# A streaming softmax: loads and stores in two queues without a fixed order, and four slots of twelve rows in place of six of eight

## The chip, the cores and the metric

The kernel runs on one core of one Trainium2 chip. The metric is the time of one execution in microseconds (us) on the device. The core has several engines with their own instruction streams: here VectorE (DVE in the profile), ScalarE (ACT) and SyncE (SP), which only issues transfers and waits. Transfers between the main memory (HBM) and the on-chip memory (SBUF, 128 partitions) are issued by an engine into its queue and carried out by the core's 16 DMA engines.

## The reference

The input is 32 x 512 rows of 1024 float32 numbers, 64 MiB, and a temperature of 0.5. Each row is replaced by its softmax:

```python
scaled = x / temperature
shifted = scaled - np.max(scaled, axis=-1, keepdims=True)
exp_x = np.exp(shifted)
return (exp_x / np.sum(exp_x, axis=-1, keepdims=True)).astype(np.float32)
```

Every number is read once and written once: 67.11 MB in, 67.11 MB out.

## The kernel before

The 16384 rows are dealt over the 128 partitions, 128 rows to each. A *row* below means one row in every partition: 128 x 1024 float32, 4 KiB in each partition. The data stand in one tile, `ring`, with room for 48 rows (`RING`, line 14), 192 KiB in each partition. A load brings `LOADS[i]` rows (line 10): 16 loads of 8 rows, 4096 KB each, so the ring has six slots. In each partition a load is one contiguous piece of 32 KiB, in memory and on the chip (`dram`, line 103). A store writes the same piece back (`STORES`, line 12). All work is done in place in the ring.

The computation goes by groups of four rows (`GROUP`, line 16), two groups to a load. For a group g:

- `maximum` (line 109): VectorE waits for the load, if g is the first group of it, and takes the largest number of each row (line 113).
- `shift` (line 120): VectorE multiplies the four maxima by -2, the bias of the exponential (line 123).
- `exponential` (line 127): ScalarE computes exp(2x + bias) of the four rows, one instruction for each, and sums them as it goes (line 131).
- `invert` (line 141): VectorE takes the reciprocals of the four sums (line 144).
- `divide` (line 146): VectorE multiplies the four rows by them (line 150), and counts up the semaphore `scaled`.

VectorE's order is written out at the end: maximum and shift of group g, then invert and divide of group g-1. So the last division of a piece comes behind the first maximum of the next piece, which waits for the next load.

All transfers are issued by SyncE, in an order that `_queue` (line 31) writes out ahead of time. It begins with six loads, one for each slot. From then on load i needs the slot of an earlier piece, and so must wait until the store of that piece has landed (line 165 behind the waits on `stored`). Ahead of such a load the list has the stores up to that piece and `AHEAD` = 2 further ones, each of which waits for the division of its last group (line 171 behind the wait on `scaled`). In the steady part store and load alternate in the one queue. After the last load come the remaining stores, and SyncE then waits until all have landed (line 176).

Of the kernel before, what the change touches and what calls it, by code (L numbers as in the profile page):

```python
# [1 line left out]

# [4 lines left out]

LOADS = [8] * 16  # L10

STORES = [[8]] * 16

RING = 48

GROUP = 4

AHEAD = 2


def _places(loads, ring):
    places, p = [], 0
    for k in loads:
        if p + k > ring:
            p = 0
        places.append(p)
        p += k
    return places


def _queue(loads, stores, places, ahead):

    flat = [(i, n) for i, ks in enumerate(stores) for n in range(len(ks))]
    last = {i: n for n, (i, _) in enumerate(flat)}
    order, given = [], 0
    for i, k in enumerate(loads):
        over = [
            b
            for b in range(i)
            if places[b] < places[i] + k and places[i] < places[b] + loads[b]  # L40
        ]
        after = max((last[b] for b in over), default=-1)
        while given <= after + ahead and after >= 0 and flat[given][0] < i:
            order.append(("store", given, None))
            given += 1
        order.append(("load", i, after))
    order += [("store", n, None) for n in range(given, len(flat))]
    return order


@with_exitstack
def kernel(
    ctx: ExitStack,
    tc: tile.TileContext,
    x: bass.AP,
    temperature: bass.AP,
    out: bass.AP,
):
    nc = tc.nc
    f32 = mybir.dt.float32  # L60
    scale = 1.0 / float(temperature)
    extreme = mybir.AluOpType.max if scale > 0 else mybir.AluOpType.min

    P = 128
    xf = x.flatten_outer_dims()
    of = out.flatten_outer_dims()
    n, d = xf.shape
    assert sum(LOADS) * P == n

    places = _places(LOADS, RING)  # L70
    first = [sum(LOADS[:i]) for i in range(len(LOADS))]
    total = sum(LOADS)

    pool = ctx.enter_context(tc.tile_pool(name="data", bufs=1))
    ring = pool.tile([P, RING, d], f32, name="ring")
    top = pool.tile([P, total], f32, name="top")
    bias = pool.tile([P, total], f32, name="bias")
    sums = pool.tile([P, total], f32, name="sums")
    recip = pool.tile([P, total], f32, name="recip")


    parts = []
    for i, ks in enumerate(STORES):
        j = 0
        for k in ks:
            parts.append((i, places[i] + j, first[i] + j, k))
            j += k
        assert j == LOADS[i]

    groups, part_end = [], []  # L90
    for i, s, r, k in parts:
        for a in range(0, k, GROUP):
            groups.append((i, s + a, r + a, min(GROUP, k - a)))
        part_end.append(len(groups))

    loaded = [tc.alloc_semaphore(f"loaded{i}") for i in range(len(LOADS))]
    stored = [tc.alloc_semaphore(f"stored{i}") for i in range(len(parts))]
    topped, biased, summed, inverted, scaled = (
        tc.alloc_semaphore(name)
        for name in ("topped", "biased", "summed", "inverted", "scaled")  # L100
    )

    def dram(t, r, k, i):

        block = t[P * first[i] : P * (first[i] + LOADS[i]), :]
        block = block.rearrange("(p k) d -> p k d", p=P, k=LOADS[i])
        return block[:, r - first[i] : r - first[i] + k, :]

    def maximum(g):
        i, s, r, k = groups[g]  # L110
        if g == 0 or groups[g - 1][0] != i:
            nc.vector.wait_ge(loaded[i], 16)
        nc.vector.tensor_reduce(  # L113
            out=top[:, r : r + k],
            in_=ring[:, s : s + k, :],
            axis=mybir.AxisListType.X,
            op=extreme,
        ).then_inc(topped, 1)

    def shift(g):  # L120
        i, s, r, k = groups[g]
        nc.vector.wait_ge(topped, g + 1)
        nc.vector.tensor_scalar_mul(  # L123
            bias[:, r : r + k], in0=top[:, r : r + k], scalar1=-scale
        ).then_inc(biased, 1)

    def exponential(g):
        i, s, r, k = groups[g]
        nc.scalar.wait_ge(biased, g + 1)
        for a in range(k):  # L130
            ins = nc.scalar.activation(  # L131
                ring[:, s + a, :],
                ring[:, s + a, :],
                mybir.ActivationFunctionType.Exp,
                bias=bias[:, r + a : r + a + 1],
                scale=scale,
                accum_out=sums[:, r + a : r + a + 1],
            )
        ins.then_inc(summed, 1)

    def invert(g):
        i, s, r, k = groups[g]
        nc.vector.wait_ge(summed, g + 1)
        nc.vector.reciprocal(recip[:, r : r + k], sums[:, r : r + k]).then_inc(inverted, 1)  # L144

    def divide(g):
        i, s, r, k = groups[g]
        nc.vector.wait_ge(inverted, g + 1)
        for a in range(k):
            ins = nc.vector.tensor_scalar_mul(  # L150
                ring[:, s + a, :], in0=ring[:, s + a, :], scalar1=recip[:, r + a : r + a + 1]
            )
        ins.then_inc(scaled, 1)

    done_to = -1
    with tc.tile_critical():  # L156

        for kind, i, after in _queue(LOADS, STORES, places, AHEAD):
            if kind == "load":
                for b in range(after + 1):  # L160
                    if b > done_to:
                        nc.sync.wait_ge(stored[b], 16)
                done_to = max(done_to, after)
                s, r, k = places[i], first[i], LOADS[i]
                nc.sync.dma_start(
                    out=ring[:, s : s + k, :], in_=dram(xf, r, k, i)
                ).then_inc(loaded[i], 16)
            else:
                l, s, r, k = parts[i]
                nc.sync.wait_ge(scaled, part_end[i])  # L170
                nc.sync.dma_start(
                    out=dram(of, r, k, l), in_=ring[:, s : s + k, :]
                ).then_inc(stored[i], 16)
        for b in range(len(parts)):
            if b > done_to:
                nc.sync.wait_ge(stored[b], 16)

        for g in range(len(groups)):
            exponential(g)


        for g in range(len(groups) + 1):
            if g < len(groups):
                maximum(g)
                shift(g)
            if g > 0:
                invert(g - 1)
                divide(g - 1)


# [1 line left out]
_INS = ['x', 'temperature']  # L192
_OUTS = [((32, 512, 1024), 'float32')]

_NUMBERS = {'temperature': 0.5}


# [26 lines left out]
```

## Time and profile before

Six runs took 321.31 to 323.24 us, with a median of 321.93. The profiled execution took 322.32 us; its span, from the first to the last instruction, is 320.5 us.

| what | value |
|---|---|
| profiled execution, span | 322.32 us, 320.5 us |
| VectorE busy | 235.4 us (73%) |
| ScalarE busy | 149.6 us (47%) |
| DMA queue q1 | 134.22 MB, 97.8% of 16 engines' span |
| maximum, 4 rows (line 113) | 32 of 4415 ns |
| exponential, one row (line 131) | 128 of 1137 ns |
| division, one row (line 150) | 128 of 749 ns |
| load, from issue to landing | 16, median 49.3 us |
| store, from issue to landing | 16, median 40.4 us |

Busy time of an engine counts its computing instructions. The share of a DMA queue is the time its packets took on the 16 DMA engines together, against 16 times the span. From issue to landing counts also the time in which a transfer stands in the queue behind others.

### The profile page before, as it was taken

How to read it: one execution, taken by the hardware profiler on the slowest of the kernel's cores; microseconds unless marked ns; L12 is line 12 of the kernel's file. 1: busy time of each engine (PE TensorE's matmuls, PEld its weight loads, DVE VectorE, ACT ScalarE, POOL GpSimd, SP SyncE). 2: the span in 40 equal slices, each digit the busy share in tenths (PEclk: the TensorE clock that was granted, in tenths of full speed). 3: DMA queues.
4: the chain of work that ended last, by engine and by line, in shares of the span. 5: the costliest groups of instructions: out<-in, count | busy, mean ns of one | idle time of the engine just before them, and what ended most of it. 6: DMA issues, size and time to landing. Idle time of an engine off the chain costs nothing.

```text
span 320.5 us, 568 instructions
## 1 busy us (share of the span) xinstructions
DVE 235.4 (73%) x224; ACT 149.6 (47%) x257; POOL 0.2 (0%) x4
## 2 busy tenths in 40 slices
DVE  0399999999996957939679395893948949498300
ACT  1076666665555551635526255262552625546000
POOL 0000000000000000000000000000000000000000
DMA  8999999999999999999999999999999999999992
GB/s 323 417 438 438 417 454 422 380 439 450 409 450 425 425 417 433 442 417 438 425 425 454 413 433 434 425 442 425 425 447 417 433 433 433 438 438 417 450 417 94
DMA packets 4612, 134.25 MB, mean 419 GB/s; under 512 B 512, under 2 KB 512, under 8 KB 512
## 3 DMA queue, kind: packets, MB, share of 16 engines
q1 hardware_dynamic: 4608, 134.22, 97.8%
q14 instruction: 4, 0.03, 0.0%
HBM read 67.11 MB, written 67.11 MB: 419 GB/s over the span
## 4 chain that ended last, share of the span: by engine, by line
DMA 55%; DVE 30%; another core or an unknown queue 5%; ACT 3%; issue 0%; SPq 0%
DMA ring<-in_x_dram 32%; DMA out_dram<-ring 24%; DVE top L113 18%; DVE ring L150 11%; ACT ring L131 3%; DVE bias L123 1%; DVE recip L144 0%; SPq L219 0%; SPq L156 0%
## 5 line engine op out<-in xcount | busy, mean ns | idle before, releaser
L131 ACT ACTIVATE ring<-ring,bias 128x1024 f32<-128x1024 f32 x128 | 145.4, 1137 | 146.6 <-DVE bias L123 146.6
L113 DVE TENSOR_REDUCE top<-ring 128x4 f32<-128x4096 f32 x32 | 141.3, 4415 | 60.4 <-DMA ring<-in_x_dram 60.4
L150 DVE TENSOR_SCALAR ring<-ring,recip 128x1024 f32<-128x1024 f32 x128 | 87.7, 749 | 1.1
L131 ACT ACTIVATION_READ_ACCUMULATOR ring<-ring,bias 128x1 f32 x128 | 23.9, 187 | 0.0
L144 DVE RECIPROCAL recip<-sums 128x4 f32<-128x4 f32 x32 | 5.5, 171 | 2.0 <-ACT ring L131 2.0
L123 DVE TENSOR_SCALAR bias<-top 128x4 f32<-128x4 f32 x32 | 5.4, 170 | 1.1
L131 ACT ACT_TABLE_LOAD x1 | 1.3, 1283 | 0.9 <-SPq L156 0.9
L205 POOL MEMSET const-bfloat16-1.0<- 128x1 bf16 x1 | 0.1, 101 | 0.0
L205 POOL MEMSET const-uint8-127<- 128x1 uint8 x1 | 0.1, 101 | 0.0
L205 POOL MEMSET const-float32-0.0<- 128x1 f32 x1 | 0.1, 98 | 0.2 <-issue 0.2
L205 POOL MEMSET const-float32-1.0<- 128x1 f32 x1 | 0.1, 98 | 0.0
## 6 DMA issues: line engine op xcount, KB each, us to landing
ring<-in_x_dram SPq DMA_DIRECT2D x16, 4096.0 KB, 49.3
out_dram<-ring SPq DMA_DIRECT2D x16, 4096.0 KB, 40.4
```

The source lines that it names most:

```text
L113: nc.vector.tensor_reduce(out=top[:, r : r + k], in_=ring[:, s : s + k, :], axis=mybir.AxisListType.X, op=extreme,).then_inc(topped, 1)
L123: nc.vector.tensor_scalar_mul(bias[:, r : r + k], in0=top[:, r : r + k], scalar1=-scale).then_inc(biased, 1)
L131: ins = nc.scalar.activation(ring[:, s + a, :], ring[:, s + a, :], mybir.ActivationFunctionType.Exp, bias=bias[:, r + a : r + a + 1], scal ...
L144: nc.vector.reciprocal(recip[:, r : r + k], sums[:, r : r + k]).then_inc(inverted, 1)
L150: ins = nc.vector.tensor_scalar_mul(ring[:, s + a, :], in0=ring[:, s + a, :], scalar1=recip[:, r + a : r + a + 1])
L205: nc = _bacc.Bacc("TRN2", target_bir_lowering=False, num_devices=1)
```

## The change

Both the queues and the sizes of the pieces are changed. The loads are now ten of twelve rows and one of eight, with stores to match: 48 KiB in each partition, four slots in the ring of 48 rows. The list in one order (`_queue`, `AHEAD`) is gone. SyncE issues the loads alone, each one as soon as the store of the piece that held its slot has landed. ScalarE issues the stores, each one in its own instruction stream behind the exponentials of the next group, after a wait for the divisions of the piece. VectorE's instructions and their order stay as they are; a load of twelve rows has three groups of four.

```diff
-LOADS = [8] * 16
-
-STORES = [[8]] * 16
+LOADS = [12] * 10 + [8]
+
+STORES = [[12]] * 10 + [[8]]
 
 RING = 48
 
 GROUP = 4
-
-AHEAD = 2
...
-def _queue(loads, stores, places, ahead):
...
+    def load(i):
+        nonlocal free_to
+        s, r, k = places[i], first[i], LOADS[i]
+
+        for n, (l, s1, r1, k1) in enumerate(parts):
+            if l < i and s1 < s + k and s < s1 + k1 and n > free_to:
+                for b in range(free_to + 1, n + 1):
+                    nc.sync.wait_ge(stored[b], 16)
+                free_to = n
+        nc.sync.dma_start(out=ring[:, s : s + k, :], in_=dram(xf, r, k, i)).then_inc(
+            loaded[i], 16
+        )
+
+    def store(n):
+        l, s, r, k = parts[n]
+        nc.scalar.wait_ge(scaled, part_end[n])
+        nc.scalar.dma_start(out=dram(of, r, k, l), in_=ring[:, s : s + k, :]).then_inc(
+            stored[n], 16
+        )
+
+    free_to = -1
     with tc.tile_critical():
-
-        for kind, i, after in _queue(LOADS, STORES, places, AHEAD):
...
-        for g in range(len(groups)):
-            exponential(g)
+        for i in range(len(LOADS)):
+            load(i)
+        for b in range(free_to + 1, len(parts)):
+            nc.sync.wait_ge(stored[b], 16)
+
+
+        for g in range(len(groups) + 1):
+            if g < len(groups):
+                exponential(g)
+            for n in range(len(parts)):
+                if part_end[n] == g:
+                    store(n)
```

More of the change, by code (lines that the diff above doesn't have):

```diff
@@ L28, in _places @@
     return places
-def _queue(loads, stores, places, ahead):
[L33 to L48, printed above, removed]
 @with_exitstack
@@ L153, in divide @@
         ins.then_inc(scaled, 1)
-    done_to = -1
-    with tc.tile_critical():
-        for kind, i, after in _queue(LOADS, STORES, places, AHEAD):
[L159 to L176, printed above, removed]
-        for g in range(len(groups)):
-            exponential(g)
+    def load(i):
[16 more added lines that the diff above has]
+    free_to = -1
+    with tc.tile_critical():
+        for i in range(len(LOADS)):
[8 more added lines that the diff above has]
+                    store(n)
         for g in range(len(groups) + 1):
```

## The prediction

> **What bounds the kernel now.** I read first the whole page, then the windows by stage, then SyncE's waits and the chain that ended last, and last the moments at which the trace says each of the 16 DMA engines finished its share of each transfer.
>
> ```profile
> span 320.5 us, 568 instructions
> ...
> DVE 235.4 (73%) x224; ACT 149.6 (47%) x257; POOL 0.2 (0%) x4
> ...
> DMA  8999999999999999999999999999999999999992
> ...
> q1 hardware_dynamic: 4608, 134.22, 97.8%
> ...
> HBM read 67.11 MB, written 67.11 MB: 419 GB/s over the span
> ```
>
> The reader is to see a row of 9s: the 16 DMA engines are busy 97.8% of the span, VectorE 73%, ScalarE 47%. All transfers are in one queue, q1. Cut by stage (columns: window, its length, then busy time of VectorE, ScalarE, GpSimd, clock, DMA share, GB/s):
>
> ```profile
> 0.00:13.30 13.30, 0.04 (x1) 1.28 (x1) 0.20 (x4) 1.00 0.88 355
> 13.30:62.00 48.70, 48.07 (x44) 30.06 (x53) 0.00 (x0) 1.00 1.01 429
> 62.00:250.00 188.00, 148.40 (x142) 94.09 (x164) 0.00 (x0) 1.00 1.00 431
> 250.00:301.00 51.00, 38.86 (x40) 24.17 (x42) 0.00 (x0) 1.00 1.00 431
> 301.00:320.50 19.50, 0.00 (x0) 0.00 (x0) 0.00 (x0) 1.00 0.67 289
> ```
>
> From 13.3 to 301 us the DMA share is 1.00, and the rate is the same when almost only loads run (429), when both kinds alternate (431) and when almost only stores run (431). Only the two ends have room: 1.6 us of 13.3 at the front, 19.5 x 0.33 = 6.4 us at the back. The median 32 KiB packet takes 1213 ns and each DMA engine carries 256, so 310.5 us of the 320.5 are plain transfer.
>
> The 6.4 us at the back are explained by the engines' own finishing times. In the first load they spread over 0.7 us; the spread stays 0.7 up to 62 us (loads alone), grows to 5.2 us by 242 us in the stretch where loads and stores alternate (2.1 at 122 us, 3.0 at 143, 3.7 at 182, 5.2 at 242), and stays 5.2 to the end (stores alone). At the end twelve engines are within 0.8 us of the first, the other four 2.3, 3.9, 3.9 and 5.2 us behind. So ten turns from load to store cost the worst engine 4.5 us, 0.45 each, and the mean engine (14.2 us of growth over 16 engines) 0.09 each; the best lost nothing. The run ends with the worst engine.
>
> Of the waits, SyncE's own (engine, line, what for: us in total, times, longest):
>
> ```profile
> SPq L171 <- DVE ring L150: 259.8, 16, 29.0
> SPq L165 <- DMA out_dram<-ring: 27.4, 9, 9.8
> ...
> ```
>
> And from the chain that ended last (start, us, what):
>
> ```profile
> 280.37 0.02 issue
> 280.39 4.43 DVE top L113
> ...
> 287.87 4.34 DVE top L113
> ...
> 297.32 2.74 DVE ring L150 x4
> ```
>
> SyncE waits mostly for VectorE to finish rows for a store, and little for a slot. The last load lands at 280.37; VectorE gives out store 14 at 287.9 and the last store at 300.1, while older stores keep the DMA engines busy (store 13 lands at 299.7, store 14 at 309.4). No compute is exposed.
>
> **The change part by part.** The sum is made against the profiled execution: 322.32 us, span 320.5 (1.8 lie around it); it is 0.4 above the median of 321.93, so I add differences to the median.
>
> *Bytes.* Unchanged, 134.22 MB: 310.5 us on each DMA engine remain.
>
> *Fewer, longer packets.* 22 transfers in place of 32, 8 packets each per DMA engine: 176 in place of 256. No row shows a 48 KiB packet. The fixed part of a packet is bounded by the smallest packets in the trace, 7 to 9 ns: 80 fewer save 0 to 0.7 us, and ten fewer completion writes of 9 ns 0.1. I take -0.7.
>
> *First piece half as long again.* Load 0 lands 4 packets x 1.213 = 4.85 us later, 18.1 instead of 13.2; VectorE starts later by that. Store 0 was issued 19.7 us after load 0's landing with two groups; a third adds 7.4 (4.34 + 0.17 + 0.09 + 2.74 and gaps), so about 46. The four loads already queued occupy the DMA engines until 3.5 + 4 x 14.55 = 61.7: hidden, 0.
>
> *Stores on ScalarE.* 11 issues of 0.33 us. Ahead of each, ScalarE waits for the division of the last group; behind it queues the exponential of the next group but one, which needs a maximum (4.34) and a shift (0.17) that VectorE does after that same division. The wait ends 4.5 us before the exponential could start, so wait and issue cost 0. But the store now also stands behind the exponential of the next piece's first group: it goes out 4.43 + 0.2 + 4.64 = 9.3 us after the next load's landing, not after 7.4. In the middle this is covered by the store ahead of it.
>
> *Loads on SyncE.* No longer queued behind stores. A slot is free when its store has landed; four slots, with a period of 29.1 us per piece (two transfers of 14.55). With equal shares, a transfer beside another takes 29 us. In the cycle of a slot: loading 29, waiting for the next load and its first group 29 + 9.3 (the division order puts the last division of a piece behind the maximum of the next), storing 29, latencies some 4: about 100 of the 116.4 us of four periods. So loads and stores stay queued. Worked through at equal shares, load 4 is issued 2 us after load 3 lands (a store is running), and every later load about 6 us before its predecessor lands. No idle DMA time: 0.
>
> *The end.* After the last load lands, store 9 can start 10.3 us later (9.3, plus 1.0 from issue to first packet, as for load 0, issued at 0.94 and first moving at 1.95). At equal shares store 8 has then about 12 us left: covered by 2 us. The last store follows 10.5 us after store 9, which takes 14.6: covered. If the cover were gone, all of the 10.3 would show.
>
> *Turns between loads and stores.* This is the term that decides. With two queues every DMA engine alternates packet by packet whenever both have work: the packets of loads 4 to 10 and about half of load 3, some 60 turns instead of 10. No row shows a packet turn. Bounds: the best engine's 0, giving -4.5 us (the lag disappears), and the worst engine's 0.45 x 60 = 27, giving +22.5. Twelve of sixteen engines lie near the lower end, so I take the mean engine's 0.09, raised to 0.13 because a landing waits for the worst of 16: 60 x 0.13 = 7.8, against 4.5 now: +3.3. The raise is a choice.
>
> Sum: -0.7 - 0.1 + 3.3 = +2.5. Span 323.0; 321.93 + 2.5 = **324.4 us**, 0.8% slower.
>
> In the Trainium skill, "DMA: Bandwidth & Descriptors", Issuing engines are not separate DMA queues, says that transfers issued from different engines run on the same 16 DMA engines and interleave, and that only the sequencer's issue time is saved; by it the turns would be free and the sum -0.8 or, with the lag gone, -5.3. The trace, with one queue, cannot show it. The same page, Queues, rings and completion order, has each DMA engine go round the queues packet by packet; that would give equal shares. No row of this case shows that either.
>
> **The rivals.** 0.3% (1 us) is about what a measurement of this kernel can tell from no change.
>
> *A, the forecast: packet turns cost.* For: lag grows only where both kinds run. Against: twelve engines lose next to nothing. Price 0.10 to 0.25 a turn: 321.93 + 0.7 = 322.6 up to 321.93 + 9.7 = 331.6.
>
> *B, stores are favoured and the end is bare.* If the DMA engines serve stores ahead of loads, store 8 is gone when the last load lands, and only stores 9 and 10 are left, with 10.3 us of idle before them: 320.5 + 10.3 - 0.8 less the lag that the idle hides (up to 4.5) is 325.5 to 330.0, so 327 to 331. It decides once the backlog of store at the last landing is below 10.3 us per engine; at equal shares it is 12. Nothing in one queue's trace speaks to shares.
>
> *C, faster: the lag belongs to transfers, not packets.* If a turn costs only where one transfer's last packets meet the next transfer's first ones in all engines at once, as the whole-transfer turns do now, seven mixed loads instead of ten give 7 x 0.45 = 3.2: -1.3 - 0.8, so 319.8; with no lag at all, 316.6. For: fast engines alternate at full rate, and their packets in the middle of a transfer keep 1213 ns. Against: nothing shows interleaved packets free. This decides below 0.08 a turn.
>
> *D, nothing measurable.* DMA bound before and after, lag as before: 321.1 to 322.
>
> **How the numbers follow.** A 0.40 (0.05 of it within 0.3%), B 0.16, C 0.34 (0.02 within), D 0.07, and 0.03 for something slower still, such as loads held back by worse lag. Faster 0.32, same 0.05 + 0.02 + 0.07 = 0.14, slower 0.35 + 0.16 + 0.03 = 0.54. The range goes from C with most of the lag gone (317.5) to A at 0.25 a turn (332); outside are some 0.08 of C below and 0.08 of A, B and the rest above. The forecast's own range is 322.6 to 331.6.
>
> **What would show it.** Two queues in the list, each with about half the busy share; DMA share 1.00 from 13 to about 300 us; loads in the middle land about 29 us apart. A is right if the rate in the middle falls below 431 GB/s (425 for +2.5 us) with no idle DMA; B if the share drops below 0.7 in one stretch between the last landing and store 9; C if the middle keeps 431 and the last stretch gets shorter. The forecast is wrong if packets of both queues overlap without loss, or if a share far from equal leaves one queue empty.

## The result and the profile after

The changed kernel takes 320.39 us, the kernel before in the same comparison 321.80; the ratio is 0.9953, 95% interval 0.9939 to 0.9966. It is 0.5% faster, where 0.8% slower was forecast. The time is inside the stated range; the sign is wrong. The times of the changed kernel scatter more: 318.4 to 322.9 us, against 320.8 to 323.5 before. Two more of its 30 runs, at 324.1 and 324.4 us, count as slow (over 1.5% above the fastest) and stand outside the ratio and this range. The profiled execution took 321.58 us with a span of 319.8, so it is one of the longer ones, and shows only 0.7 us of the gain.

The page of the changed kernel:

```profile
span 319.8 us, 557 instructions
...
DVE 235.1 (74%) x224; ACT 149.6 (47%) x257; POOL 0.2 (0%) x4
...
DMA  7999999999999999999999999999999999995996
...
q1 hardware_dynamic: 1584, 67.11, 49.1%
q10 hardware_dynamic: 1584, 67.11, 48.5%
...
HBM read 67.11 MB, written 67.11 MB: 420 GB/s over the span
```

There are now two queues with half of the bytes each. The row of 9s has a dent near its end, which was not there before. By stage (columns as before: window, length, busy time of three engines, clock, DMA share, GB/s):

```profile
0.00:17.50 17.50, 0.00 (x0) 1.28 (x1) 0.20 (x4) 1.00 0.94 385
17.50:62.00 44.50, 42.96 (x38) 27.61 (x48) 0.00 (x0) 1.00 1.00 430
62.00:250.00 188.00, 149.63 (x143) 92.90 (x162) 0.00 (x0) 1.00 1.00 433
250.00:301.00 51.00, 39.58 (x40) 26.98 (x47) 0.00 (x0) 1.00 0.93 401
```

From 62 to 250 us, where loads and stores alternate packet by packet, the rate is 433 GB/s, where the kernel before had 431: alternating costs nothing. What the trace says of single packets shows why. These are four packets that follow one another on one DMA engine (start, duration in ns, queue, bytes; the trace does not name the engine, the times tell which packet follows which):

```
62364 1815 q1  49152
64176 1815 q10 49152
65987 1815 q1  49152
67799 1815 q10 49152
```

A load (q1) and a store (q10) take turns strictly, each begins 3 to 4 ns before the other's end, and a packet takes the median 1815 ns whichever kind stood before it. SyncE's waits (for what: us in total, times, longest), and below them lines of the timeline about the end of the last load (start, us, instruction):

```profile
SPq L142 <- DMA out_dram<-ring: 245.0, 7, 75.2
...
```

```profile
285.16 4.42 DVE L91 TENSOR_REDUCE top<-ring 128x4 f32<-128x4096 f32 x1 [2.62 <-DMA ring<-in_x_dram]
...
289.90 2.74 DVE L128 TENSOR_SCALAR ring<-ring,recip 128x1024 f32<-128x1024 f32 x4
...
292.10 1.13 ACT L109 ACTIVATE ring<-ring,bias 128x1024 f32<-128x1024 f32 x1
292.67 0.34 ACTq L149 DMA_DIRECT2D out_dram<-ring  x1
293.14 0.19 ACT L109 ACTIVATION_READ_ACCUMULATOR ring<-ring,bias 128x1 f32 x1
293.24 1.13 ACT L109 ACTIVATE ring<-ring,bias 128x1024 f32<-128x1024 f32 x1
```

SyncE now waits for stores alone. The last load lands at 285.14, 4.8 us later than before, and store 9 goes out 7.5 us after it, in the middle of the exponentials of the next group. Cut into 5 us, the dent is (same columns):

```profile
280.00:285.00 5.00, 2.54 (x4) 4.36 (x8) 0.00 (x0) 1.00 0.99 429
285.00:290.00 5.00, 4.77 (x4) 0.18 (x1) 0.00 (x0) 1.00 0.61 265
290.00:295.00 5.00, 5.00 (x5) 4.46 (x8) 0.00 (x0) 1.00 0.44 187
```

Fourteen of the 16 DMA engines had finished store 8 by 290.5 us (the first at 288.8) and stood idle until store 9 began at 293.6; the slowest finished store 8 at 294.2 and did not stand idle there. The last stores then land on all 16 engines within 0.3 us of each other: the idle of the fast engines has taken up the whole lag of the slow one.

### The profile page after: what moved, and what is told of

Same layout as the page of the kernel before. It is cut to its first block, busy times and chain, and to the rows that moved or that the text cites. A ratio compares the mean times of both kernels' runs of the same rounds, so it can differ in the third digit from the quotient of the medians.

```text
span 319.8 us, 557 instructions
## 1 busy us (share of the span) xinstructions
DVE 235.1 (74%) x224; ACT 149.6 (47%) x257; POOL 0.2 (0%) x4
## 4 chain that ended last, share of the span: by engine, by line
DMA 76%; DVE 14%; ACT 6%; issue 0%; SPq 0%
DMA ring<-in_x_dram 39%; DMA out_dram<-ring 37%; DVE top L91 10%; ACT ring L109 6%; DVE ring L128 3%; DVE bias L101 0%; DVE recip L122 0%; SPq L206 0%; SPq L154 0%
## 6 DMA issues: line engine op xcount, KB each, us to landing
ring<-in_x_dram SPq DMA_DIRECT2D x10, 6144.0 KB, 38.9
```

## The experiments

The times are ratios to runs of the kernel before on the same chip. One table holds what the traces say of each kernel, so that the sections can be short. *Plain* is the number of packets on a DMA engine times their median duration. *Slow* counts, over all 16 engines, packets between 60 and 260 us that took over 100 ns more than the median of their size. *Lag* is how far the 16 engines' landings of the last load lie apart.

| kernel | queues | packets | plain, us | slow | lag, us | span, us | ratio (95%) |
|---|---|---|---|---|---|---|---|
| before | 1 | 32 KiB | 310.5 | 59 | 5.2 | 320.5 | 1 |
| changed | 2 | 48 KiB | 309.8 | 33 | 7.2 | 319.8 | 0.9953 (0.9939 to 0.9966) |
| changed, again | 2 | 48 KiB | 309.8 | 31 | 3.6 | 318.1 | 0.9939 (0.9926 to 0.9952) |
| queues alone | 2 | 32 KiB | 310.5 | 7 | 3.2 | 318.0 | 0.9912 (0.9899 to 0.9925) |
| queues alone, again | 2 | 32 KiB | 310.5 | 4 | 2.0 | 316.9 | 0.9905 (0.9885 to 0.9925) |
| pieces alone | 1 | 48 KiB | 309.8 | 36 | 4.7 | 319.5 | 1.0001 (0.9991 to 1.0012) |
| pieces alone, half packets | 1 | 24 KiB | 311.4 | 37 | 3.7 | 319.2 | 0.9996 (0.9979 to 1.0012) |
| changed, half packets | 2 | 24 KiB | 311.4 | 25 | 1.6 | 317.5 | 0.9917 (0.9897 to 0.9937) |
| changed, quarter packets | 2 | 12 KiB | 314.2 | 15 | 1.1 | 318.6 | 0.9959 (0.9943 to 0.9976) |
| six rows, eight slots | 2 | 24 KiB | 311.4 | 3 | 1.9 | 317.7 | 0.9923 (0.9904 to 0.9942) |
| four rows, twelve slots | 2 | 16 KiB | 312.8 | 3 | 2.3 | 318.3 | 0.9939 (0.9915 to 0.9964) |
| end split | 2 | 48 KiB, 16 at the end | 310.0 | 55 | 7.6 | 319.7 | 0.9970 (0.9944 to 0.9996) |
| copy | 2 | 48 KiB | 309.8 | 1 | 2.7 | 316.7 | 0.9882 (0.9861 to 0.9904) |
| eight rows, four slots | 2 | 32 KiB | 310.5 | 12 | 1.9 | 322.4 | 1.0076 (1.0053 to 1.0098) |

A lag belongs to one profiled execution and varies from one to the next (the two of the changed kernel have 7.2 and 3.6); the ratio rests on all runs. Lag is also a rough measure in two queues: the next store to land has its 16 landings 5.4 us apart in the changed kernel where the last load has 7.2, and 2.1 and 1.8 with half and quarter packets where it has 1.6 and 1.1.

A simpler measure is *span* minus *plain*, all that the slowest engine loses, the two ends included. In one queue it is 10.0 us with 32 KiB packets, 9.7 with 48 and 7.8 with 24. In two queues it is 10.0 and 8.3 at 48 KiB (9.7 with the end split, 6.9 in the copy), 7.5 and 6.4 at 32 (11.9 with four slots, where all engines stand idle for a while), 6.1 and 6.3 at 24, 5.5 at 16 and 4.4 at 12.

**The queues alone.** The edit is to the changed kernel.

```diff
-LOADS = [12] * 10 + [8]
-STORES = [[12]] * 10 + [[8]]
+LOADS = [8] * 16
+STORES = [[8]] * 16
```

> The queues alone are changed: loads in SyncE's queue, stores in ScalarE's, pieces of eight rows and six slots as before. Theory P (pieces: fewer packets save their fixed 9 ns, fewer loads meet stores, so less lag on the slowest DMA engine): no gain, ratio 1.000 to the kernel before, about 321.8 us. Theory Q (the gain comes from the free order of the two queues): all of it is here, ratio 0.995, about 320.4. Theory T of the prediction (each packet turn costs the slowest engine 0.13 us): 80 turns, 321.8 - 4.5 + 10.4 = 327.7 us.

Measured 319.05 us, ratio 0.9912. The gain is here, and more than the whole change has. Theory T is out by 8.7 us; theory P, which wanted no gain, falls too.

```profile
DMA  8999999999999999999999999999999999999994
...
q1 hardware_dynamic: 2304, 67.11, 49.3%
q10 hardware_dynamic: 2304, 67.11, 48.9%
```

The queues' shares together are 98.2%, and the row has no dent: with six slots the end is covered.

**The pieces alone.** The edit is to the kernel before.

```diff
-LOADS = [8] * 16
-STORES = [[8]] * 16
+LOADS = [12] * 10 + [8]
+STORES = [[12]] * 10 + [[8]]
-AHEAD = 2
+AHEAD = 1
```

> The pieces alone are changed: twelve rows, four slots, all transfers in SyncE's queue in the written order, with AHEAD = 1 so that a load does not wait for a store that cannot go out yet. Theory P: the gain is here, 0.7 us of packets and about 1 us of lag, ratio 0.994 to 0.996, 319.9 to 320.5 us. Theory Q: only the packets' 0.7 us, ratio 0.998, 321.1 us. If four slots in one fixed order leave the DMA engines without work, it is slower than before and its DMA share in the middle falls below 1.00.

Measured 321.82 us, ratio 1.0001: not even the packets' 0.7 us is to be seen in the median. So in one queue twelve rows gain nothing, though seven loads instead of ten run beside stores. Lag does not go by the number of such loads alone.

```profile
DMA  7999999999999999999999999999999999999992
...
q1 hardware_dynamic: 3168, 134.22, 97.9%
```

The DMA engines were not short of work in the fixed order either, so missing work is not what kept the gain away.

**The changed kernel again.** No edit.

> The changed kernel once more, unedited, for another profile of it. Ratio 0.995 to the kernel before. Its span should follow the lag of the slowest DMA engine: a profile 2 us shorter than the first (319.8 us) should show a last load that lands 2 us earlier than 285.1 us, with 1815 ns packets as in the first.

Measured 319.85 us, ratio 0.9939. The span is 318.1, the last load lands at 283.3: 1.7 us less span for 1.8 us earlier. The packets take 1815 ns here too. Between these two executions the difference in span is the difference in the landing of the last load on the slowest engine.

**The end split.** The edit is to the changed kernel.

```diff
-STORES = [[12]] * 10 + [[8]]
+STORES = [[12]] * 9 + [[4, 4, 4], [4, 4]]
```

> The changed kernel with the stores of the last two pieces cut into parts of four rows, so that eight of twelve rows of piece 9 can go out before the last load has landed. In the changed kernel's profile 15 DMA engines stand idle for some 4 to 5 us before store 9. If that idle costs time, the gain is 2 us or more: ratio about 0.988 to the kernel before, 318 us. If the slowest DMA engine, which had no idle there, sets the end, nothing is gained: ratio 0.995 as for the changed kernel, while the DMA share between the last landing and the end rises from 0.44 to near 1.

Measured 320.74 us, ratio 0.997 (0.9944 to 0.9996).

```profile
280.00:285.00 5.00, 3.60 (x7) 4.15 (x7) 0.00 (x0) 1.00 0.94 406
285.00:290.00 5.00, 4.29 (x1) 0.49 (x2) 0.00 (x0) 1.00 0.95 410
290.00:295.00 5.00, 4.93 (x8) 4.63 (x8) 0.00 (x0) 1.00 0.98 419
```

The dent is filled (0.61 and 0.44 became 0.95 and 0.98), and no time is gained. The idle of the fast engines cost nothing, because the last byte waits for the slowest one, which was not idle there in the changed kernel either. The last store lands on the first engine at 313.3 and on the last at 318.3. This kernel differs from the changed one only in its last two pieces, yet its profile has 55 slow packets between 60 and 260 us, where the changed kernel has 33 and 31: with 48 KiB packets in two queues the number varies that much from one execution to the next.

**Four rows, twelve slots.** The edit is to the changed kernel.

```diff
-LOADS = [12] * 10 + [8]
-STORES = [[12]] * 10 + [[8]]
+LOADS = [4] * 32
+STORES = [[4]] * 32
```

> Two queues as in the changed kernel, pieces of four rows and twelve slots: 512 packets of 16 KiB on each DMA engine, 32 loads of which some 20 run beside stores. Fixed cost of 9 ns a packet: +3.0 us on 176 packets. Theory T (a turn costs 0.13 us on the slowest engine): about 160 turns, +13 us over the changed kernel's 60. Theory P (a load that runs beside stores costs the slowest engine some 0.4 us each): 20 loads, 8 to 9 us of lag, 5 us more than before. If lag goes by the time in which both kinds run, not by the number of loads, it stays at 4 to 5 us: about 323 us in all.

Measured 320.05 us, ratio 0.9939. The packets cost 3.0 us more, as reckoned (611 ns each, 312.8 against 309.8), yet the lag is 2.3 us. Twenty loads beside stores and over twice the turns bring less lag, not more: T and P both fall here.

**Half packets.** The edit is to the changed kernel, in loads and stores alike; `halves` views a piece in the ring as two halves. Transfers and order stay; each partition's piece lies in two places in memory, and so becomes two packets.

```diff
-        block = block.rearrange("(p k) d -> p k d", p=P, k=LOADS[i])
-        return block[:, r - first[i] : r - first[i] + k, :]
+        block = block.rearrange("(h p k) d -> p h k d", h=2, p=P, k=LOADS[i] // 2)
+        return block
...
-        nc.sync.dma_start(out=ring[:, s : s + k, :], in_=dram(xf, r, k, i)).then_inc(
+        nc.sync.dma_start(out=halves(s, k), in_=dram(xf, r, k, i)).then_inc(
```

> The changed kernel with each row piece of a partition in two halves that lie apart in memory: the same 22 transfers, 352 packets of 24 KiB in place of 176 of 48 KiB, so twice the turns. Fixed cost: 176 x 9 ns = +1.6 us. Theory T: 60 more turns, +7.8 us. Theory P: lag unchanged, since the loads are the same: +1.6 us in all, about 322.0 us. The packets should take about 910 ns.

Measured 319.32 us, ratio 0.9917. The packets take 912 ns, and plain time rises by 1.6 us as expected; the lag falls to 1.6 us, and the kernel is faster than the changed one. Doubling the turns with the transfers untouched lowers the time: the turn's price is not 0.13 us. Since the edit also shortens the packets, that a turn costs nothing rests on the packets' own times, above.

**A copy.** The changed kernel without its computation; VectorE's loop goes as well.

```diff
-        nc.scalar.wait_ge(scaled, part_end[n])
+        nc.scalar.wait_ge(loaded[l], 16)
...
-        for g in range(len(groups) + 1):
-            if g < len(groups):
-                exponential(g)
...
+        for n in range(len(parts)):
+            store(n)
```

> The changed kernel without maximum, shift, exponential, inversion and division: each store waits for its load alone, so the output is the input. It tells whether the lag of single DMA engines needs the engines' work in the ring. If VectorE and ScalarE reading and writing the ring cause the slow load packets, the lag at the last landing is below 1 us, and the span is about 315 us. If not, single loads still fall behind by some us in the stretch where both kinds run, and the span is 316 to 320 us.

Measured 318.22 us, ratio 0.9882 (0.9861 to 0.9904), span 316.7. The lag at the last load is 2.7 us, so some lag is there without any work of VectorE and ScalarE. But it stems from the first meeting of loads and stores (26 slow packets, at 17 to 25 us); between 60 and 260 us there is one slow packet, against 33 and 31 with the computation. Since without computation the stores also go out earlier and the loads stand in the queue longer (78.7 us from issue to landing, against 38.9), this does not say which of the two matters.

**Six rows, eight slots.** The edit is to the changed kernel.

```diff
-LOADS = [12] * 10 + [8]
-STORES = [[12]] * 10 + [[8]]
+LOADS = [6] * 21 + [2]
+STORES = [[6]] * 21 + [[2]]
-GROUP = 4
+GROUP = 3
```

> Two queues, 21 pieces of six rows and one of two, eight slots, groups of three rows: packets of 24 KiB, 344 on each DMA engine. If lag goes by the length of the packets (5.4 and 3.6 us at 48 KiB, 3.2 at 32, 2.1 before the end at 24, 1.6 at 16), it is about 2.2 us here, 1.0 less than with 32 KiB in two queues, for 88 more packets at 9 ns = 0.8: ratio 0.990 to 0.992, 318.6 to 319.2 us. If the number of loads beside stores counted (14 in place of 10), about 321.

Measured 319.36 us, ratio 0.9923. Lag 1.9 us, plain 0.9 us more than with 32 KiB packets: no better than the queues alone with eight rows.

**Half packets in one queue.** The kernel with the pieces alone, with the edit of the half packets.

```diff
-        block = block.rearrange("(p k) d -> p k d", p=P, k=LOADS[i])
-        return block[:, r - first[i] : r - first[i] + k, :]
+        block = block.rearrange("(h p k) d -> p h k d", h=2, p=P, k=LOADS[i] // 2)
+        return block
...
```

> The kernel with twelve-row pieces in one queue, its packets cut to 24 KiB as in the run with half packets, transfers and order unchanged. Theory L (short packets alone bring less lag): lag about 2 us in place of 4.65, less 1.6 us for 176 more packets: ratio 0.996 to 0.997, about 320.8 us. Theory I (short packets help only where loads and stores alternate packet by packet, so two queues are needed): lag stays at 4 to 5 us, and 1.6 us come on top: ratio 1.005, 323.4 us.

Measured 321.85 us, ratio 0.9996: between the two theories. Slow packets are as many as with long ones (37 and 36), and the lag is 3.7 in place of 4.7 us, against 1.6 us for the additional packets. Short packets alone gain no time. They do lose less: span minus plain falls from 9.7 to 7.8 us, and the additional packets take that back. In two queues the same edit lowers it from 10.0 and 8.3 to 6.1 and gave some 0.3% on the changed kernel. So a good part of what short packets bring does not need two queues.

**Quarter packets.** As the half packets, with four parts (`h=4`).

> The changed kernel with each piece in four parts: the same 22 transfers in two queues, 704 packets of 12 KiB (8 KiB for the last piece) on each DMA engine. Fixed cost against 176 packets: 528 x 9 ns = +4.8 us. If lag falls further with packet length, to about 1 us, 321.5 us or ratio 0.998 to 0.999; if the lag of the half packets was chance and is 3.6 to 5.4 us again, 324 to 325 us, ratio 1.007 to 1.010.

Measured 320.41 us, ratio 0.9959. The lag is the smallest of all, 1.1 us, and the packets' fixed part takes the gain back: plain 314.2 us.

**Eight rows with four slots.** The edit is to the kernel with the queues alone.

```diff
-RING = 48
+RING = 32
```

> Two queues and pieces of eight rows as in the run with the queues alone, but a ring of 32 rows: four slots, as many as the changed kernel has, with 32 KiB packets. In the changed kernel a load lands 39 us after its issue, with eight rows and six slots 52. If the slow load packets in the middle (32 and 30 between 60 and 260 us in the two profiles of the changed kernel, 6 with eight rows and six slots) come from having only four slots, some 20 to 40 are seen here, and the slowest DMA engine ends 4 to 5 us behind. If they come from the length of the packets, fewer than 10. Fewer rows in the ring can also leave the DMA engines without work for some 4 us in all; ratio 0.992 to 1.010.

Measured 324.27 us, ratio 1.0076 (1.0053 to 1.0098). There are 12 slow packets, ten of them before 70 us: closer to the 7 of six slots than to 33, just outside the line of ten that was drawn. The lag is 1.9 us. So neither four slots nor a short load queue (26.6 us from issue to landing) brings the slow packets back with 32 KiB pieces. The time is lost at the end:

```profile
62.00:250.00 188.00, 140.41 (x134) 90.53 (x158) 0.00 (x0) 1.00 1.00 432
250.00:301.00 51.00, 40.26 (x36) 23.20 (x40) 0.00 (x0) 1.00 0.92 398
301.00:322.40 21.40, 6.84 (x12) 4.64 (x8) 0.00 (x0) 1.00 0.77 331
```

With 32 rows in the ring the stores still to do run out before the last divisions. Here the idle is on all 16 engines, and it costs.

**The queues alone, again.** No further edit.

> The kernel with two queues, eight rows and six slots once more, unedited: ratio 0.991 to the kernel before, and again fewer than 10 slow load packets between 60 and 260 us, with the slowest DMA engine 2 to 4 us behind before the last store.

Measured 318.68 us, ratio 0.9905; 4 slow packets, lag 2.0 us. Leaving the copy aside, this one, stores in ScalarE's queue with the old six slots of eight rows, is the fastest kernel tried: 0.9% below the kernel before and 0.3 to 0.5% below the changed one. Half packets (0.9917) and six rows (0.9923) lie within its interval (0.9885 to 0.9925).

## Why the prediction was wrong

- **What bounds the kernel** held: 134.22 MB at the DMA engines' rate, and a slowest engine that ends last. In every experiment the rate in the middle was 430 to 435 GB/s.
- **Fewer, longer packets**, -0.7 us: right as transfer time, though with the pieces alone it did not show in the median. 611, 912, 1213 and 1815 ns for 16, 24, 32 and 48 KiB lie on one line with a fixed part of 9 ns; 309.8 against 310.5 us.
- **First piece** and **the loads**: right. Load 0 landed at 18.45 (18.1 reckoned) and store 0 went out at 45.6 (46). Load 4 went out 3 us after load 3 had landed, and load 5 some 6 us before load 4 did on the first engine; the DMA share was 1.00.
- **Stores on ScalarE**: the delay behind the exponentials was wrong. ScalarE issued the store 7.5 us after the landing, not 9.3: the store went out at 292.67, while the third of the four exponentials that stand before it ran and 0.57 us before the fourth began. At the end this keeps store 9 just in time for the slowest engine, which finished store 8 at 294.2 when store 9 began at 293.6. Had it gone out 1.8 us later, that engine would have stood idle for some 1.2 us (an estimate).
- **The end**: the cover of 2 us was reckoned for engines in step. On the slowest it was about nothing, on the others minus 4 to 5 us, and filling that idle gained nothing. Of rival B one half is real: idle on all engines before the last stores costs time, as the ring of 32 rows shows. The other half, stores served ahead of loads, did not happen; the shares were equal.
- **Turns between loads and stores**, +3.3 us: this step failed. It took the lag of the kernel before, 0.45 us for each turn of a whole transfer on the worst engine and 0.09 on the mean, for a price of a turn, chose 0.13 from them, and multiplied by 60. The turn from packet to packet costs nothing (1815 ns and no gap), and the kernels with more turns lose less: with quarter packets, at four times the turns, all that the slowest engine loses is 4.4 us, under 0.02 for each of 240 turns. That the first profile's lag of 7.2 us lies near the 7.8 reckoned is chance: the second profile has 3.6, and the store that lands next has 5.4 and 3.6, against 5.2 before. The packets have no gaps and a steady median, so the lag must come from single slow packets; in the second profile of the changed kernel the three engines that do not stand idle near the end, the slowest, carry 17 of the 31. At 32 KiB they are far fewer in two queues (7 and 4 against 59), at 24 KiB fewer (25, or 3 with six rows, against 37), but at 48 KiB not (33, 31 and 55 against 36).
- **Rival C** had the sign and nearly the size (319.8 against 320.39), and was right that the turn of a packet is free, but its reason for the gain fails. Seven mixed loads instead of ten gained nothing in one queue, and ten of them in two queues gained more than seven.

Shown: the gain comes with the edit of the queues, at every packet length tried both ways (0.9% at 32 KiB, 0.5 to 0.6% at 48, some 0.8% at 24), and the larger pieces give part of it back. That edit does three things at once: it puts the stores in a second queue, issues them from ScalarE, and frees the order of loads and stores. A kernel with two queues in the written order was not tried, so which of the three brings the gain is open.

Open, too, is what makes a packet slow: single ones take up to 1.4 us longer than their neighbours. Most are loads (all of them in one queue), but with half packets 9 of 25 and with quarter packets 11 of 15 are stores. In two queues, pieces of twelve rows have 15 to 55 such packets and pieces of four to eight rows 3 to 7, or 12 with four slots. Neither packet length alone (the copy has one at 48 KiB) nor the number of slots explains it, and a larger ring with 48 KiB pieces was not tried. At 48 KiB the number of slow packets does not explain the gain either.

## What to carry to other kernels

Where the DMA engines are full from end to end, look at when each of the 16 finishes: the slowest engine is the time, and idle on the others is free. A lag counted per turn of whole transfers is no price per packet turn; vary the turns before multiplying by them. Change queue and piece size one at a time: here one gained 0.9%, the other gained nothing in one queue and cost 0.3 to 0.5% in two.

## What was unexpected

Loads in one queue and stores in another alternated strictly, one packet each, at no cost, and with shorter packets the engines lay closer together, though not at every step: lags of 3.6, 7.2 and 7.6 us at 48 KiB, 3.2 and 2.0 at 32, 1.9 and 1.6 at 24, 2.3 at 16 and 1.1 at 12. Against that stand 9 ns for each packet, and the best of the kernels tried lie between, at 32 and 24 KiB. A transfer that stands behind exponentials in ScalarE's stream went out while they ran, with one of them still to begin.
